# A three-layer fp32 network in one launch: its schedule built with the timeline simulation switched on

## The chip, the cores and the metric

The kernel runs on one core of a Trainium2 chip, in one launch. The metric is the device time of that launch in microseconds (us), the median of several runs. The engines are called as in the profile: PE (TensorE, the matmuls) with its weight loads PEld, DVE (VectorE), ACT (ScalarE), POOL (GpSimd) and SP (SyncE), which issues DMAs.

## The reference

`x` is one batch of 512 tokens of width 1024, all in float32. Three different blocks follow each other:

- Block 1: 16 learned tokens are put in front (528 tokens). `h += 0.5 * swiglu(rmsnorm(h))`; then a mixer whose two halves read the same normed input: forgetting attention ("fox", 16 heads of 64, softmax over `q k^T / 8` plus the difference of two cumulative sums of `log_sigmoid` gates) and retention (4 heads). `h += (sigmoid(ga) * fox @ w_o_fox + sigmoid(gb) * ret @ w_o_ret) @ w_out`; then a second swiglu FFN.
- Block 2: a gMLP mixer and a Mamba2 state-space mixer (chunks of 64 tokens: `y = (C B^T * decay) xdt + C state`), gated, projected and added; then an FFN with a causal convolution of 3 taps.
- Block 3: native sparse attention ("NSA": 8 heads; a compressed branch, and two branches with a band of position biases) beside an RWKV7 recurrence (8 heads of 64: in each chunk of 64 tokens a triangular system is solved, then `state = decay * state + update`), their outputs concatenated and projected; then the convolution FFN again.

## The kernel before, in words

Everything lies feature-major in SBUF: 128 features by 512 (or 528) tokens to a tile. Each projection weight is streamed from HBM once, 128 output features at a time, by `Ctx.wunit` (L236 to L248): SP starts a DMA of 128 x 1024 floats, ACT copies it to the rounded half `wh` (L240), DVE subtracts to get the rest `wl` (L244); the pool holds two of each. `Ctx.mm3` (L250 to L252) makes each product of three matmuls, `wh*xh`, `wh*xl` and `wl*xh`. Such a streamed matmul is the kernel's bulk work and its filler: it waits only for its weights and an accumulator.

In the four FFNs there is nothing but these. In the mixers they are mixed with work in dependent chains:

- fox, per pair of heads: scores on PE (L648 to L651), a masked exponential with row sums on DVE and ACT (L653, L660), transposes on PE (L673), the split of the transposed probabilities into `fph` (ACT, L282) and `fpl` (DVE, L287), and the products with the values (PE, L679 with `fph`, L680 with `fpl`). Beside them the next heads' q and k are projected, normed (`hrs`, `hsq`: ACT L488, L489, L455) and split (`fk0h`, `fk1h`: ACT L305, L307).
- SSD (block 2), per chunk: transposes and splits (L443, L444, L1084), score products (L1076), `E` (DVE, L1109) into the product L1112, outputs and states (L1118, L1123).
- RWKV, four pairs of heads: the triangular systems in six levels of small products (`heads`, L1711; `level`), then 8 steps for each pair, 32 in all (`steps`: PE L1809, ACT L1811, PE L1816 and L1819, DVE L1824, PE L1831 and L1834, DVE L1837). A step needs the state of the last.
- NSA, 16 units of one head, one branch: scores (PE L1535, L1536), bias and row maximum (DVE L1537), exponential (ACT L1543), scaling (POOL L1547), transposes (PE L1555), split (`ph` on ACT, `pl` on DVE) and value products (PE L1560, L1561).

The program text only gives the instructions and their dependences. What sets the order on each engine is the list scheduler of the tile framework: it holds all instructions of the context, runs them through a model of the machine, and appends to each engine's in-order queue the instruction that the model finds next. So the model decides in what order a streamed matmul, a chain's product, an ACT copy and a DVE subtraction follow each other on their engines; in the trace each engine's instructions come in the order of its own queue. Which streamed matmuls may stand between which chain instructions is also bounded by dependences and by the buffers. The chain of one RWKV step in the text:

```python
nc.tensor.matmul(rr[64 * s:64 * s + 64], ml[:, s, n, :64], vs[:, s, n], start=True, stop=True)  # L1809
nc.scalar.activation(rs_, rr, AF.Copy)                                                          # L1811
nc.tensor.matmul(sa[h], xt[h, n], rs_[h], start=True, stop=True)                                # L1819
nc.vector.tensor_copy(vs[:64, s, n], sa[64 * s:64 * s + 64])                                    # L1824
nc.tensor.matmul(ds[:, 64 * s:64 * s + 64], bk[:, s, n], vs[:, s, n], start=True, stop=True)    # L1834
nc.vector.tensor_add(s0, ds.rearrange("p (s d) -> p s d", s=2), s0)                             # L1835
nc.vector.tensor_mul(to, s0, wend[:, :, n:n + 1].to_broadcast([64, 2, 64]))                     # L1837
```

## Time and profile before

| what | value |
|---|---|
| median of 3 runs (lowest, highest) | 3429.2 us (3425.64, 3435.23) |
| profiled execution: its own time, its span | 3428.05 us, 3426.2 us |
| mean granted clock of PE | 0.988 |
| busy share PE, PEld | 97%, 79% |
| busy share DVE, ACT, POOL | 56%, 41%, 21% |
| DMA | 298.61 MB, 87 GB/s |

The span is the time from the first to the last instruction of the profiled execution; the 1.85 us between it and that execution's own time lie outside the instructions. PE's busy time counts each matmul from its start to a modelled end, and neighbours overlap, so a stretch in which PE is busy throughout can still hold more or fewer matmuls per microsecond: the distance from one start to the next tells that. The stages by time, from PE's instructions: FFN 1 to about 390 us, fox and retention to about 1110, FFN 2 to 1462, block 2's mixer to about 2064, FFN 3 to about 2494, RWKV about 2587 to 2867, NSA to 3031, the output projection and FFN 4 to the end.

### The profile page before, as it was taken

Reading aid. Unit: us, or ns where it says so; the run is one execution under the profiler, and the core shown is the slowest. Engines: PE = TensorE matmul, PEld = TensorE weight load, DVE = VectorE, ACT = ScalarE, POOL = GpSimd, SP = SyncE. Lnnn points to the kernel's source line nnn. Section 1 sums busy time; section 2 is a strip of 40 time slices with the busy share of each in tenths; the row PEclk is TensorE's granted clock in tenths of the full one; section 3 lists DMA queues with packets and bytes.
Section 4 is the critical chain, followed back from the end, with each engine's and each line's share of the span. In section 5 each row is a group of like instructions: output and inputs, shape, how many; then the busy total and the mean of one; then the engine's idle time right before and its main releaser. Section 6 shows DMA issues by size and latency. Waiting matters only on the chain. (4 is left out here: it accounts for less than half of the span.)

```text
span 3426.2 us, 48101 instructions
## 1 busy us (share of the span) xinstructions
PE 3309.6 (97%) x19089; PEld 2717.3 (79%) x19089; DVE 1932.8 (56%) x3242; ACT 1404.0 (41%) x2474; POOL 712.4 (21%) x748
## 2 busy tenths in 40 slices
PE   8999999999999999999999999999999998999999
PEld 8999977778877888876777778788876766778887
DVE  4433366655754433268777564566446656766642
ACT  3222366653433322235555233444333434754431
POOL 2110133332122111112121231111113222421100
PEclk9999999999999999999999999999999999999999
DMA  3223222232223232323332322223331012122332
GB/s 120 90 93 88 86 85 78 69 97 95 66 86 102 92 99 90 96 94 85 106 100 86 111 81 98 92 93 98 104 115 34 31 46 87 41 64 96 98 101 91
DMA packets 89601, 298.61 MB, mean 87 GB/s; under 512 B 10711, under 2 KB 11351, under 8 KB 89120
## 3 DMA queue, kind: packets, MB, share of 16 engines
q1 hardware_dynamic: 76896, 260.70, 23.7%
q0 software_dynamic: 6416, 23.80, 2.4%
q10 hardware_dynamic: 6064, 11.03, 1.0%
q8 instruction: 150, 2.46, 0.3%
q14 instruction: 75, 0.61, 0.1%
HBM read 288.02 MB, written 7.47 MB: 86 GB/s over the span
## 5 line engine op out<-in xcount | busy, mean ns | idle before, releaser
L250 PE MATMUL mm<-zh,wh 128*128 128x512 f32 (+1 forms) x3296 | 1189.8, 361 | 20.2 <-ACT zh L291 8.4
L252 PE MATMUL mm<-zh,wl 128*128 128x512 f32 (+1 forms) x3296 | 1189.0, 361 | 3.8 <-DVE wl L244 3.7
L251 PE MATMUL mm<-zl,wh 128*128 128x512 f32 (+1 forms) x3296 | 1180.2, 358 | 3.1 <-DVE zl L292 3.1
L240 ACT ACTIVATE wh<-w 128x1024 fp32r<-128x1024 f32 (+2 forms) x523 | 523.8, 1001 | 1086.6 <-PE mm L251 759.0
L244 DVE TENSOR_TENSOR wl<-w,wh 128x1024 fp32r<-128x1024 f32 (+2 forms) x523 | 627.6, 1201 | 400.1 <-ACT wh L240 392.3
L250 PEld LDWEIGHTS mm<-zh,wh 128*128 128x128 f32 x3296 | 622.8, 189 | 115.6 <-issue 10.6
L251 PEld LDWEIGHTS mm<-zl,wh 128*128 128x128 f32 x3296 | 623.6, 189 | 100.6 <-DVE zl L292 4.1
L252 PEld LDWEIGHTS mm<-zh,wl 128*128 128x128 f32 x3296 | 622.6, 189 | 100.2 <-DVE wl L244 6.9
L250 PE MATMUL mm<-hh,wh 128*128 128x512 f32 (+1 forms) x880 | 308.5, 351 | 0.0
L251 PE MATMUL mm<-hl,wh 128*128 128x512 f32 (+1 forms) x880 | 308.3, 350 | 0.0
L252 PE MATMUL mm<-hh,wl 128*128 128x512 f32 (+1 forms) x880 | 307.6, 350 | 0.0
L251 PEld LDWEIGHTS mm<-hl,wh 128*128 128x128 f32 x880 | 165.6, 188 | 23.3
L250 PEld LDWEIGHTS mm<-hh,wh 128*128 128x128 f32 x880 | 165.5, 188 | 23.3
L252 PEld LDWEIGHTS mm<-hh,wl 128*128 128x128 f32 x880 | 165.6, 188 | 23.1
L382 POOL TENSOR_TENSOR ta<-ta,rs 128x264 f32<-128x264 f32 (+1 forms) x66 | 86.0, 1316 | 395.8 <-ACT ta L381 395.8
L334 POOL TENSOR_TENSOR acc<-acc,ta 128x512 f32<-128x512 f32 (+1 forms) x49 | 85.2, 1739 | 345.7 <-ACT ta L333 345.3
L1000 POOL TENSOR_TENSOR cv<-cv 128x512 f32<-128x512 f32 x44 | 57.6, 1309 | 434.0 <-DVE cv L981 397.6
L981 DVE SCALAR_TENSOR_TENSOR cv<-ta,vec,cv 128x510 f32<-128x510 f32 (+1 forms) x176 | 132.0, 753 | 3.2 <-ACT cv L978 0.3
L384 DVE TENSOR_TENSOR tb<-mm,ta 128x264 f32<-128x264 f32 (+1 forms) x66 | 32.8, 519 | 141.5 <-PE mm L252 137.7
L380 DVE TENSOR_TENSOR ta<-mm,rs 128x264 f32<-128x264 f32 (+1 forms) x66 | 32.5, 518 | 108.3 <-PE mm L252 108.3
L995 DVE TENSOR_TENSOR ta<-mm,rs 128x512 f32<-128x512 f32 x88 | 60.3, 687 | 57.9 <-PE mm L252 57.8
L282 ACT ACTIVATE hh<-cv 128x512 fp32r<-128x512 f32 x44 | 27.8, 632 | 144.7 <-POOL cv L1000 144.7
(592 smaller groups left out, 4645.3 us busy)
## 6 DMA issues: line engine op xcount, KB each, us to landing
w<-in_w_up_dram SPq DMA_DIRECT2D x176, 512.0 KB, 3.5
w<-in_w_in_dram SPq DMA_DIRECT2D x160, 512.0 KB, 3.5
w<-in_w_dn_dram SPq DMA_DIRECT2D x64, 512.0 KB, 3.5
w<-in_w_dn_dram SPq DMA_DIRECT2D x32, 384.0 KB, 3.1
w<-in_w_out_dram SPq DMA_DIRECT2D x16, 512.0 KB, 3.5
aB<-acum_d POOLq DMA_DIRECT2D x16, 512.0 KB, 5.9
w<-in_w_pb_dram SPq DMA_DIRECT2D x32, 256.0 KB, 2.9
negc<-negc_d POOLq DMA_DIRECT2D x8, 528.0 KB, 4.1
```

Of the source, the lines that this page charges most:

```text
L240: nc.scalar.activation(h_, w_, AF.Copy)
L244: nc.vector.tensor_sub(l_, w_, h_.bitcast(F32))
L250: nc.tensor.matmul(ps, wh, xh, start=start, stop=False)
L251: nc.tensor.matmul(ps, wh, xl, start=False, stop=False)
L252: nc.tensor.matmul(ps, wl, xh, start=False, stop=stop)
L334: nc.gpsimd.tensor_tensor(acc, acc, q, op=ALU.add)
L380: nc.vector.tensor_mul(ta, a, rs[:, c])
L382: nc.gpsimd.tensor_tensor(ta, ta, rs[:, c], op=ALU.mult)
L384: nc.vector.tensor_mul(tb, b, ta)
L981: nc.vector.scalar_tensor_tensor(y[:, d:], x[:, :T - d], w(i), y[:, d:], op0=ALU.mult, op1=ALU.add)
L995: nc.vector.tensor_mul(x, p, rs)
L1000: nc.gpsimd.tensor_tensor(y[1], y[1], y[0], op=ALU.mult)
```

## The change

One argument is given to the context in which the whole program is built:

```diff
--- before.py
+++ after.py
@@ -2006,7 +2006,7 @@
         feed[f"in_{name}_dram"] = a
         D[name] = nc.dram_tensor(f"in_{name}_dram", a.shape, mybir.dt.from_np(a.dtype), kind="ExternalInput").ap()
     out = nc.dram_tensor("out_0_dram", (8, 128, 512), F32, kind="ExternalOutput").ap()
-    with tile.TileContext(nc) as tc:
+    with tile.TileContext(nc, schedule_with_timeline_sim=True) as tc:
         program(tc, D, vec, out)
     act_tables(nc)
     r = run_bass_kernel_spmd(nc, [feed], core_ids=[0])
```

It changes the model that the list scheduler runs: a timeline simulation of the engines takes the place of the default one. No tile, pool, dependence, shape or operation differs. PE has 15806 rows of instructions before and 15812 after (neighbours that differ in nothing but a slice are one row). Of PE's 17413 instructions 7022 stand at another place than before, of DVE's 3244 2106, of ACT's 2374 1474, of POOL's 753 223, and of SP's 536 4, each by one place. In the four FFNs the order on PE is the same. The consecutive stretches of streamed matmuls (L250 to L252) on PE, counted over the whole program as runs, go from 451 to 269: in fox from 149 to 102, in SSD from 46 to 58, in RWKV from 110 to 24, in NSA from 67 to 9.

The first place is ACT at the end of a fox head. `fph` are the probabilities' high halves for which L679 waits, `hrs` and `hsq` belong to the norm of a later head, `fk` is that head's k, `wh` a weight tile. Before:

```order
L488 ACTIVATE hrs_6860<-s_6861,eps0_291 128x512
L282 ACTIVATE fph_6883<-t_6878 128x512
L489 ACTIVATE hrs_6860<-hrs_6860 128x512
L282 ACTIVATE fph_6893<-t_6889 128x384
L455 ACTIVATE hsq_6722<-hrs_6860 128x512
L240 ACTIVATE wh_7028<-w32_7027 128x1024
L282 ACTIVATE fph_6902<-t_6899 128x256
```

After:

```order
L240 ACTIVATE wh_7247<-w32_7246 128x1024
L282 ACTIVATE fph_6883<-t_6878 128x512
L282 ACTIVATE fph_6893<-t_6889 128x384
L488 ACTIVATE hrs_6860<-s_6861,eps0_291 128x512
L489 ACTIVATE hrs_6860<-hrs_6860 128x512
L455 ACTIVATE hsq_6722<-hrs_6860 128x512
L305 ACTIVATE fk0h_6748<-fqt_6638 64x528
L307 ACTIVATE fk0h_6748<-fqt_6638 64x528
L305 ACTIVATE fk1h_6754<-fqt_6638 64x528
L307 ACTIVATE fk1h_6754<-fqt_6638 64x528
L282 ACTIVATE fph_6902<-t_6899 128x256
L282 ACTIVATE fph_6910<-t_6908 128x128
```

Before, one `hrs` or `hsq` instruction stands between two `fph`, a weight copy right ahead of `fph_6902`, and the `fk` copies are already done. After, a weight copy of a later tile goes ahead of `fph_6883`, and the norm's three instructions and the four `fk` copies all stand between `fph_6893` and `fph_6902`.

The second place is PE in the triangular systems of RWKV (L1711; L1654, L1657 and L1630 belong to the features of a later pair, `mm_22344` is streamed work). Before:

```order
L250 MATMUL mm_22344<-zh2_21318,wh_22346 128x512
L251 MATMUL mm_22344<-zl2_21319,wh_22346 128x512
L1711 MATMUL s_22088<-xt_21768,ys0_22062 64x32 x8
L1711 MATMUL s_22097<-xt_21784,ys1_22075 64x32 x8
L252 MATMUL mm_22344<-zh2_21318,wl_22347 128x512
L250 MATMUL mm_22344<-zh3_21328,wh_22346 128x512
L251 MATMUL mm_22344<-zl3_21329,wh_22346 128x512
L1711 MATMUL t_22108<-id64_21502,xt_21768 64x64 x8
L1711 MATMUL t_22118<-id64_21502,xt_21784 64x64 x8
```

After:

```order
L1711 MATMUL t_22064<-x0_21767,ls_22060 64x32 x8
L1711 MATMUL t_22077<-x1_21783,ls_22073 64x32 x8
L1711 MATMUL s_22088<-xt_21768,ys0_22062 64x32 x8
L1711 MATMUL s_22097<-xt_21784,ys1_22075 64x32 x8
L1711 MATMUL t_22108<-id64_21502,xt_21768 64x64 x8
L1654 MATMUL s_22130<-acc_21514,w2a_21506 128x512
L1711 MATMUL t_22118<-id64_21502,xt_21784 64x64 x8
L1657 MATMUL s_22133<-acc_21514,w2a_21506 128x512
L1711 MATMUL t_22154<-x0_21767,ls_22150 64x32 x8
```

The streamed matmuls that stood among the small products are gone from here: 40 of them (`mm_22026` and `mm_22344`) now come ahead of the first L1711 of the stage. Of the 31 distances from one step's L1819 to the next, 3 hold no streamed matmul before, and 21 after. In the last steps of the stage 72 streamed matmuls now stand that came in the NSA stage before (`mm_25061`, `mm_25149`, `mm_25260`).

The third place is PE in an NSA unit (`ph`, `pl` and `p` are the unit's probabilities, `mm_26631` is streamed work of the output projection). Before:

```order
L250 MATMUL mm_26631<-nh4_21485,wh_26633 128x512
L251 MATMUL mm_26631<-nl4_21486,wh_26633 128x512
L1583 MATMUL o_26347<-pch_25985,vcd11_24511 128x512
L252 MATMUL mm_26631<-nh4_21485,wl_26634 128x512
L1560 MATMUL o_26148<-ph_26155,v01_24517 128x512
L1535 MATMUL s_26219<-kh01_24515,qs1_25794 128x512
L1536 MATMUL s_26219<-kl01_24516,qs1_25794 128x512
L250 MATMUL mm_26631<-nh5_21487,wh_26633 128x512
L1561 MATMUL o_26148<-pl_26156,v01_24517 128x512
```

After:

```order
L1560 MATMUL o_26148<-ph_26155,v01_24517 128x512
L1535 MATMUL s_26219<-kh01_24515,qs1_25794 128x512
L1536 MATMUL s_26219<-kl01_24516,qs1_25794 128x512
L1561 MATMUL o_26148<-pl_26156,v01_24517 128x512
L1555 MATMUL t_26171<-cst_247,p_25988 128x128 x2
L1560 MATMUL o_26148<-ph_26165,v01_24517 128x384
L1583 MATMUL o_26347<-pch_25985,vcd11_24511 128x512
L1561 MATMUL o_26148<-pl_26166,v01_24517 128x384
L1560 MATMUL o_26148<-ph_26174,v01_24517 128x256
```

The streamed matmuls have left the units: before, 40 of the 64 L1561 stand ahead of the stage's last streamed matmul, after, none; of the 64 L1535 groups 51 before, 9 after. The stage holds 203 streamed matmuls before and 144 after.

## Rows read from the trace of the kernel before

**Rows 1.** The page, busy time of each engine, share of the span, instructions

```profile
PE 3309.6 (97%) x19089; PEld 2717.3 (79%) x19089; DVE 1932.8 (56%) x3242; ACT 1404.0 (41%) x2474; POOL 712.4 (21%) x748
```

**Rows 2.** Windows: us, then busy of PE, PEld, DVE, ACT, POOL, clock, DMA, GB/s

```profile
...
592.18:630.64 38.46, 36.38 (x227) 30.50 (x227) 25.85 (x61) 24.44 (x55) 14.62 (x25) 1.00 0.24 78
1204.00:1290.00 86.00, 86.00 (x376) 70.21 (x375) 34.20 (x39) 24.09 (x30) 14.37 (x8) 1.00 0.30 97
1462.00:1862.00 400.00, 378.81 (x1833) 294.68 (x1832) 300.76 (x419) 211.19 (x404) 79.95 (x63) 0.97 0.31 93
...
```

**Rows 3.** Timeline of PE in a dense FFN: start, us, engine, instruction

```profile
...
3200.31 0.39 PE L250 MATMUL mm<-zh,wh 128*128 128x512 f32 x1
3200.53 0.39 PE L251 MATMUL mm<-zl,wh 128*128 128x512 f32 x1
...
```

**Rows 4.** Timeline of PE, streamed matmuls among the RWKV ones

```profile
...
2821.66 0.50 PE L250 MATMUL mm<-zh,wh 128*128 128x512 f32 x1
2822.00 0.39 PE L251 MATMUL mm<-zl,wh 128*128 128x512 f32 x1
...
2822.69 0.39 PE L251 MATMUL mm<-zl,wh 128*128 128x512 f32 x1
2823.01 0.34 PE L1809 MATMUL o<-h,ml 128*64 128x64 f32 x4
...
```

**Rows 5.** The waits of PE in fox: us in total, times, longest

```profile
...
PE o L680 <- DVE fpl L287: 7.5, 12, 1.2
...
PE o L679 <- ACT fph L282: 4.7, 13, 0.5
...
```

**Rows 6.** ACT by form in one fox head: count, busy, mean ns, idle before

```profile
L240 ACT ACTIVATE wh<-w 128x1024 fp32r<-128x1024 f32 x4 | 4.3, 1063 | 1.1 <-PE mm L251 1.1
...
L305 ACT ACTIVATE fk0h<-fqt 64x528 fp32r<-64x528 f32 x1 | 0.6, 643 | 1.4 <-DVE fqt L593 1.4
...
```

**Rows 7.** The waits of PE in the SSD and gMLP stage

```profile
...
PE o L1112 <- DVE E L1109: 8.0, 3, 3.1
...
PE t L443 <- ACT tb L282: 7.2, 5, 2.4
...
```

**Rows 8.** Windows of the RWKV stage, columns as in Rows 2

```profile
...
2587.09:2867.18 280.09, 262.74 (x3254) 188.43 (x3254) 175.71 (x430) 108.58 (x274) 80.74 (x109) 0.96 0.13 40
2790.00:2820.00 30.00, 29.66 (x580) 24.20 (x578) 12.79 (x42) 14.40 (x42) 12.09 (x22) 1.00 0.24 75
2850.00:2860.00 10.00, 6.75 (x65) 4.69 (x64) 5.46 (x26) 4.90 (x18) 0.00 (x0) 1.00 0.17 49
2860.00:2870.00 10.00, 5.83 (x45) 4.18 (x44) 8.65 (x19) 5.26 (x12) 5.21 (x4) 0.52 0.11 28
2870.00:2880.00 10.00, 10.00 (x44) 6.45 (x43) 4.01 (x10) 3.70 (x8) 1.26 (x1) 0.79 0.13 34
...
```

**Rows 9.** Timeline of PE at the RWKV entry, with the idle time before

```profile
...
2587.09 1.96 PE L1711 MATMUL s<-ar,b 64*64 64x128 f32 x32 [1.72 <-POOL b L1689]
...
2593.23 0.68 PE L1711 MATMUL t<-id,xt 64*64 64x64 f32 x16 [2.60 <-DVE xt L1724]
...
```

**Rows 10.** The waits of PE in the RWKV steps

```profile
...
PE o L1831 <- DVE h L1824: 4.8, 8, 1.1
...
PE o L1809 <- DVE h L1837: 3.1, 4, 1.7
...
PE o L1819 <- ACT rsb L1811: 2.5, 3, 1.7
...
```

**Rows 11.** Windows of the NSA stage, columns as in Rows 2

```profile
...
2867.18:3030.70 163.52, 147.57 (x740) 110.89 (x741) 119.33 (x362) 102.50 (x268) 56.82 (x90) 0.95 0.15 51
2912.00:3030.70 118.70, 104.28 (x551) 79.50 (x551) 89.46 (x292) 80.85 (x226) 45.98 (x78) 0.96 0.10 35
...
```

**Rows 12.** PE by form in the NSA units, 2912 to 3030.7 us

```profile
...
L250 PE MATMUL mm<-nh,wh 128*128 128x512 f32 x24 | 9.9, 414 | 0.0
L1560 PE MATMUL o<-ph,v 128*128 128x512 f32 x16 | 8.7, 542 | 3.2 <-ACT ph L282 2.9
...
```

## The prediction, made before the changed kernel ran

> **What bounds the kernel now.** I read the page's busy times first, then windows stage by stage, then PE's timeline and its list of waits. PE is busy 3309.6 us, 97% of the span, and no other engine comes to 60% [rows 1]; so the span is PE's queue, and what is not PE's is about 117 us of idle time (3426.2 - 3309.6). The change takes nothing out of PE's queue and puts nothing in. It can gain only where PE stands still or where its matmuls follow each other more slowly than they could, and it can lose by adding such places.
>
> In the FFNs neither exists: a window of one holds 86.00 us of PE in 86.00 [rows 2], and streamed matmuls start 0.23 us apart [rows 3]. The order there is unchanged, so I cost these stages at nothing. All the movement is in the mixers. There a second loss hides in the busy time. In the run of streamed matmuls between two small ones in RWKV, the first holds PE 0.34 us until the next start and the last 0.32, while the two between go at 0.23 [rows 4]. So a run of streamed matmuls costs about 0.11 + 0.09 = 0.20 us beyond its matmuls, wherever one starts and ends. There are 451 such runs before and 269 after.
>
> [...]
>
> **The change part by part.** Everything is set against the profiled execution: 3428.05 us, a span of 3426.2 and 1.85 outside. It lies 1.15 us under the median of the runs shown.
>
> Fox, 8 pairs of heads. One pair takes 38.46 us, of which PE is idle 38.46 - 36.38 = 2.1 [rows 2]; the waits are for `fpl` and `fph`, in all 7.5 us in 12 and 4.7 in 13, none over 1.2 [rows 5]. In the new order a weight copy of 1.06 us goes ahead of the first `fph`, and four `fk` copies of 0.64 us, 2.6 in all, stand before the third [rows 6]. L679 and L680 are queued behind one another on PE, and behind them the filler that could have covered the wait. Walking the two queues by these durations I get PE waits of 0.55 (the accumulator's copy, late by the same queue), 0.55, 1.0, 0.8 and 2.45 us, 5.35 in place of 2.1: +3.3 for each pair. Against it stand 149 - 102 = 47 fewer runs at 0.20 us, 9.4 us or 1.2 for a pair. That is +2 for a pair, **+16 us**. Bounds: -10 (the runs saved, no new wait) and +30 (the waits, and only the bubbles of the runs that lie beside no wait).
>
> SSD and gMLP. PE is idle 400 - 378.81 = 21 us here [rows 2], of which 8.0 lie before L1112 and 7.2 before L443 [rows 7]. The first group of chunks gets its filler better spread, the second stands with almost none in its first three chunks; runs rise from 46 to 58, 12 x 0.20 = +2.4. I take **-4 us**, some of the 15 us of these two waits covered less the runs, and keep -20 (all covered and a little more) and +15 (the same waits again in the second group).
>
> RWKV, 280.09 us, of which PE is idle 17 [rows 8]. Four pieces:
> 110 - 24 = 86 fewer runs at 0.20: -17.2. The forty streamed matmuls that now stand ahead of the first L1711 (9.2 us) give POOL's `b` and DVE's `xt` the time for which PE waited 1.72 and 2.60 us [rows 9]: -4.3. The 72 streamed matmuls that come into the last steps fill the two windows where PE is busy 6.75 and 5.83 of 10 us, 7.4 us idle [rows 8]: -7.4. On the other side, 21 - 3 = 18 more steps have no streamed matmul in them. The waits inside a step are 10.4 us in 15 now (4.8, 3.1, 2.5), 0.7 each [rows 10]. But in the new order small products of the next pair still stand between, and the window at 2790, which has ten streamed matmuls among 580 instructions and is busy 29.66 of 30 us, shows that these alone nearly suffice [rows 8]. I take half a wait, 0.4 us a step: +7.2. Together **-22 us**. Bounds: -41, if the steps lose nothing and a run saves 0.34 instead of 0.20; and +66, if in each of the 18 the longest waits seen all come (1.1 + 1.7 + 1.7, and one more of 0.8 at the ends, 5.3 x 18 = 95, less the 29 saved).
>
> NSA, 163.52 us, 118.7 of it 16 units at 7.42 us [rows 11, 12]. The units hold 72 streamed matmuls, 16.6 us at 0.23 or 1.03 a unit: without them a unit is 6.4 us. DVE is busy 89.46 us in the units, 5.6 for each: the floor. The 58 runs that vanish save up to 0.7 a unit, but the chain's own waits come bare. I take 6.25 us, so 16 x 6.25 = 100, and the 144 streamed matmuls that remain, nearly all ahead of the chain, 33 us: 133, and 4 for a stretch at half clock (next paragraph), 137. Like for like (59 matmuls, 13.6 us, have left the stage) before is 163.5 - 13.6 = 150: **-13 us**. Bounds: 16 x 5.6 + 33, -27; and 16 x 7.4 + 33 + 7, +8.
>
> The clock. Between 2850 and 2870 PE's busy share falls to 67 and 58%, and the granted clock goes to 0.52, then 0.79 in the next ten microseconds of full work [rows 8]: that is 1.2 GHz for a while, at a loss of 4.8 + 2.1 = 7 us of granted clock. The mixers' own windows show 0.95 to 1.00 [rows 2, 8, 11]. This can appear wherever PE loses its filler, and here it disappears in one place and may come in another; I took 4 us of it into NSA.
> The Trainium skill ("TensorE: Matmul & The Clock Gate", section "HAM oscillation — how this bites in real kernels") says the same with a sharper edge: idle stretches that come back with each tile of work drop PE to half clock each time, so the price is paid once for each gap and not once for the stage. The trace shows one such drop here. By that rule the chain stretches without filler would be the slow case below.
>
> DVE, ACT, POOL, SP. They work as much as before; SP's DMA issues move by one place, and with DVE busy only 34.20 of 86 us in an FFN [rows 2] I cost that at nothing.
>
> Sum: +16 - 4 - 22 - 13 = -23. The span becomes 3403.2, the time **3405 us**.
>
> **The rivals.**
> First, slower: the filler was cover, and without it the chains stand bare. The place is the 18 RWKV steps. A clean step takes some 6.7 us (the window at 2790); at the pace of the window at 2850, where PE is busy 63% instead of 99, it takes 3.8 us more. Half of that, 2.0 a step, is 36 us, less the 29 saved +7; with fox at +16, SSD at -4 and NSA at its upper bound of +8 it makes +27, 3455 us. It decides from the point where a bare step costs (23 + 7)/18 = 1.7 us instead of 0.4. For it: 21 of 31 steps bare. Against it: in the window at 2790 small work alone keeps PE at 99%.
>
> Second, it cancels: fox at +30, SSD at 0, RWKV at -22, NSA at -8 (units of 6.55 us). That is 0, 3428 us. For it: fox's `fph` queue is the plainest change that I can read, and the gains are sums of small pieces.
>
> Third, a larger gain: DVE-bound NSA units (-27), RWKV without new waits (-36, near its bound), SSD -4, fox +5 since its filler slides into the waits. Together -62, 3366 us. [...] Against it: in the units PE waits for ACT and POOL as well, 3.2 us on the first `ph` alone [rows 12].
>
> That the change does nothing is out: the orders differ.
>
> **How the numbers follow.** My forecast 0.43, the slow rival 0.25, the cancelling one 0.17, the large gain 0.15. About 0.3% (10 us) is what a measurement of this kernel can tell from no change. The forecast's own range is 3388 to 3418. Faster is the forecast and the large gain, less 0.01 for a forecast that comes out just short: 0.57. Within 0.3% is the cancelling case, 0.17. Slower is the slow rival and the 0.01: 0.26. The range goes from a little beyond the large gain to the slow rival, **3355 to 3455**; beyond it lie RWKV at its upper bound and fox and NSA both at theirs.
>
> **What would show it.** Right: in the fox pair a longest wait of PE on `fph` of about 2.5 us in place of 0.5, and the pair at 40.5 us; RWKV with PE idle under 15 us and no long wait at its entry; the stretch of bare NSA units at 6.2 to 6.3 us each, with no streamed matmul in it; FFNs unchanged to the microsecond. Wrong: a granted clock near 0.5 over much of the NSA units or of the RWKV steps; PE waits on `vs` (L1824) or the state (L1837) two or three times as long as now; fox waits that stay where they are, since then the model put each instruction where the chip has it ready.

## The result and the profile after

The changed kernel takes 3510.8 us (median of 4 runs, 3506.18 to 3513.02) against 3429.05: 1.0237 times the time before, 95% interval 1.0224 to 1.025. The profiled execution's span grew from 3426.2 to 3507.1 us. The forecast was 3405 in a range of 3355 to 3455, so direction and range were both missed.

The page's busy times after, and its row of the granted clock over 40 slices, to be held against [rows 1]:

```profile
PE 3342.9 (95%) x19089; PEld 2763.0 (79%) x19089; DVE 1949.0 (56%) x3242; ACT 1399.5 (40%) x2474; POOL 698.5 (20%) x748
...
PEclk9999999989989999999999999999998877999999
```

The same 19089 matmul records take 33 us more of PE, and PE stands still for 164 us and not 117. The clock, which was at 9 tenths or more in each of the 40 slices before, dips in fox and over the stretch of RWKV and NSA.

Stage by stage, from the start times of PE's instructions. I split each stage by adding up, over the trace, the time from each matmul's start to the next one's start. "Idle" is the time from the end of all matmuls so far to the next start, where that is more than 0.1 us; "streamed" is the rest behind an L250, L251 or L252, "small" the rest behind all others. A matmul with such a gap behind it is thus counted to its modelled end, and one without it only to its neighbour's start, so that more gaps also raise "small" or "streamed".

| stage (ends with) | before | after | difference | idle | streamed (matmuls) | small |
|---|---|---|---|---|---|---|
| start to fox (first L626) | 446.8 | 446.1 | -0.7 | -5.4 | +5.8 | -0.5 |
| fox (last L756) | 295.7 | 321.5 | **+25.8** | +12.9 | -0.3 (1051 to 1032) | +13.1 |
| retention, first part (last L820) | 197.1 | 200.4 | +3.3 | -8.0 | +12.1 (1046 to 1101) | -0.8 |
| rest of retention, FFN 2, start of block 2 (first L1164) | 576.0 | 574.5 | -1.5 | +6.3 | -8.5 | +0.7 |
| SSD (last L1118) | 331.7 | 321.8 | **-9.8** | -7.1 | -0.4 | -2.4 |
| gMLP (last L1285) | 188.2 | 184.7 | -3.5 | +1.5 | -3.6 | -1.4 |
| FFN 3 to RWKV's features (first L1654) | 535.3 | 528.9 | -6.4 | -3.3 | -3.1 | 0.0 |
| features (first L1711) | 16.4 | 23.2 | +6.8 | -2.3 | +9.1 (48 to 88) | 0.0 |
| RWKV (last L1819) | 289.7 | 344.4 | **+54.7** | +35.2 | -10.4 (325 to 344) | +29.9 |
| NSA (last L1561) | 152.5 | 165.1 | **+12.6** | +15.8 | -15.1 (203 to 144) | +12.0 |
| projection, FFN 4 | 392.7 | 392.2 | -0.5 | +1.5 | -2.0 | 0.0 |
| sum | | | +80.8 | +47.1 | -16.3 | +50.6 |

So 47 us are new idle time and 51 us lie behind small matmuls, while the streamed ones became cheaper, as fewer runs should make them. Streamed matmuls that change their stage carry 0.23 us each with them [rows 3]; with that taken off, fox lost 30.2 us, RWKV 50.3 and NSA 26.2.

Of the small column's growth in these three (13.1, 29.9 and 12.0 us) 11.1, 10.6 and 7.8 us are matmuls with a gap behind them, of which there are 32, 52 and 47 in place of 2, 12 and 26: time of the same waits, by the way of counting. The small matmuls that others follow without a gap take 2.0, 19.3 and 4.2 us more. In RWKV 813 of those start while the clock is at 0.50, 0.090 us apart on average, and 2110 while it is at 1.00, 0.054 apart; before, 112 started at 0.50.

Three windows of the kernel before that were not shown, fox, RWKV up to its last L1819, and NSA (columns as in Rows 2):

```profile
446.80:742.50 295.70, 281.54 (x1707) 231.42 (x1704) 194.54 (x462) 184.72 (x412) 106.38 (x193) 1.00 0.24 78
...
2587.10:2876.70 289.60, 271.81 (x3295) 194.47 (x3297) 178.74 (x438) 112.19 (x282) 83.18 (x111) 0.95 0.13 40
...
2876.70:3029.20 152.50, 138.20 (x701) 104.69 (x701) 115.75 (x352) 97.72 (x257) 54.38 (x87) 0.97 0.16 53
```

And of the changed kernel: fox, SSD, RWKV, NSA, then four windows of 10 us inside RWKV:

```profile
446.10:767.60 321.50, 294.18 (x1687) 243.25 (x1686) 197.03 (x460) 185.69 (x413) 103.45 (x192) 0.93 0.22 74
1542.50:1864.30 321.80, 309.70 (x1556) 241.03 (x1555) 256.11 (x358) 184.57 (x370) 64.56 (x54) 0.99 0.32 96
2601.10:2945.50 344.40, 291.00 (x3321) 221.80 (x3320) 187.03 (x439) 117.17 (x290) 77.52 (x113) 0.82 0.11 34
2945.50:3110.60 165.10, 134.79 (x638) 100.96 (x636) 109.72 (x341) 94.03 (x249) 50.71 (x85) 0.92 0.13 44
...
2650.00:2660.00 10.00, 5.81 (x96) 5.38 (x96) 9.84 (x14) 2.25 (x6) 6.86 (x5) 0.50 0.01 2
2720.00:2730.00 10.00, 4.25 (x64) 3.91 (x65) 8.96 (x16) 3.25 (x9) 5.42 (x5) 0.50 0.00 1
2800.00:2810.00 10.00, 4.46 (x76) 4.24 (x76) 9.82 (x17) 2.47 (x7) 7.05 (x6) 0.50 0.01 2
2810.00:2820.00 10.00, 9.09 (x29) 4.02 (x30) 3.07 (x11) 3.17 (x7) 0.00 (x0) 0.50 0.00 2
```

RWKV's clock is 0.82 against 0.95, NSA's 0.92 against 0.97. The pattern in three of the short windows repeats: DVE is busy 9 to 10 of 10 us, PE 4 to 6, and the clock is 0.50 (1.2 GHz); in the window at 2810 it is still there although PE is busy 9 of 10 us again. Counted over the trace, the clock stands at 0.50 in 28 stretches, 246 us in all, against 18 and 82 us before; in RWKV in 8 stretches and 126 us against 5 and 27. The waits of PE in RWKV after:

```profile
PE o L1809 <- DVE h L1837: 13.2, 9, 3.2
PE o L1831 <- DVE h L1824: 11.3, 7, 5.1
PE o L1819 <- DVE xt L1755: 4.9, 1, 4.9
PE s L1711 <- POOL ys L1744: 2.9, 3, 1.2
```

Against [rows 10] the waits for the state (L1837) went from 3.1 to 13.2 us and those for L1824 from 4.8 to 11.3. Where the idle time lies can be read step by step. Of the 31 distances from one step's L1819 to the next, 22 in this trace hold no streamed matmul (21 in the queues), and they hold 32.8 us of idle time, 1.5 each; before, 3 such distances held 6.9. The steps with streamed matmuls in them hold 8.1 us as before (8.0), and the stretch ahead of the first step 11.9 against 2.8.

Two of the long waits show what PE waits for. DVE around 2660 us, ahead of the first step:

```profile
2651.40 2.31 DVE L1677 TENSOR_TENSOR_SCAN fx<-chunk,lw 128x512 f32<-128x512 f32 x1
2653.64 1.18 DVE L1683 TENSOR_SCALAR ar<-kk 128x8 f32<-128x8 f32 x1
2654.73 0.67 DVE L1681 SCALAR_TENSOR_TENSOR ar<-kk,ec 128x504 f32<-128x504 f32 x1
2655.32 2.81 DVE L1774 COPY wend<-ec 64x4 f32<-64x4 f32 x4
...
2659.29 1.82 DVE L1773 COPY ml<-ar 64x512 f32<-64x512 f32 x2
...
2662.68 0.29 DVE L1755 TENSOR_TENSOR xt<-s,xt 128x128 f32<-128x128 f32 x1
```

and PE at the same time:

```profile
2656.16 1.92 PE L1711 MATMUL s<-xt,ys 64*64 64x32 f32 x32
2663.03 0.48 PE L1819 MATMUL o<-rsb,xt 64*64 64x64 f32 x4 [4.94 <-DVE xt L1755]
2663.29 1.92 PE L1711 MATMUL s<-ar,b 64*64 64x128 f32 x16
2665.14 0.79 PE L250 MATMUL mm<-zh,wh 128*128 128x512 f32 x1
2665.73 0.63 PE L251 MATMUL mm<-zl,wh 128*128 128x512 f32 x1
2666.16 0.63 PE L252 MATMUL mm<-zh,wl 128*128 128x512 f32 x1
2666.59 0.49 PE L250 MATMUL mm<-zh,wh 128*128 128x512 f32 x1
```

The products for L1755 end at 2658.08. L1755, 0.29 us long, runs at 2662.68, behind features and operands of the next pair that DVE has ahead of it in its queue. L1819 waits for it 4.94 us with nothing else to do: the streamed matmuls stand behind it and one L1711 group in PE's queue, too late to fill the wait. When they come, the second and third start 0.43 us ahead of the next and not 0.23 [rows 3]; the clock stood at 0.50 since 2649.7.

Inside a step without streamed matmuls it is the same. PE, then DVE, at 2805 us:

```profile
2804.82 1.86 PE L1711 MATMUL s<-xt,ys 64*64 64x32 f32 x32
2810.17 0.47 PE L1831 MATMUL o<-lrb,h 64*64 64x64 f32 x2 [3.48 <-DVE h L1824]
```

```profile
2806.64 1.81 DVE L1773 COPY ml<-ar 64x512 f32<-64x512 f32 x2
2808.47 0.75 DVE L1694 SCALAR_TENSOR_TENSOR bo<-r,vec,k 128x512 f32<-128x512 f32 x1
2809.14 0.85 DVE L1773 COPY ml<-ar 64x512 f32<-64x512 f32 x2
2809.91 0.47 DVE L1824 COPY h<-o 64x64 f32<-64x64 f32 x2
```

The L1819 whose result L1824 copies starts at 2804.58; the copy runs at 2809.91, behind DVE's bulk work for the next pair.

### The profile page after: what moved, and what is told of

Read it like the earlier page. It is cut to its first block, busy times and chain, and to the rows that moved or that the text cites. A ratio compares the mean times of both kernels' runs of the same rounds, so it can differ in the third digit from the quotient of the medians.

```text
span 3507.1 us, 48161 instructions
## 1 busy us (share of the span) xinstructions
PE 3342.9 (95%) x19089; PEld 2763.0 (79%) x19089; DVE 1949.0 (56%) x3242; ACT 1399.5 (40%) x2474; POOL 698.5 (20%) x748
## 5 line engine op out<-in xcount | busy, mean ns | idle before, releaser
L250 PE MATMUL mm<-zh,wh 128*128 128x512 f32 (+1 forms) x3296 | 1187.3, 361 | 28.3 <-ACT wh L240 8.8
L252 PE MATMUL mm<-zh,wl 128*128 128x512 f32 (+1 forms) x3296 | 1187.2, 361 | 12.6 <-DVE wl L244 12.5
L251 PE MATMUL mm<-zl,wh 128*128 128x512 f32 (+1 forms) x3296 | 1176.6, 357 | 2.8 <-DVE zl L292 2.7
L244 DVE TENSOR_TENSOR wl<-w,wh 128x1024 fp32r<-128x1024 f32 (+2 forms) x523 | 637.7, 1220 | 418.7 <-ACT wh L240 411.6
L250 PEld LDWEIGHTS mm<-zh,wh 128*128 128x128 f32 x3296 | 623.7, 189 | 125.5 <-ACT wh L240 10.8
L252 PEld LDWEIGHTS mm<-zh,wl 128*128 128x128 f32 x3296 | 623.4, 189 | 113.2 <-DVE wl L244 15.9
L251 PEld LDWEIGHTS mm<-zl,wh 128*128 128x128 f32 x3296 | 625.4, 190 | 102.7 <-DVE zl L292 4.6
L250 PE MATMUL mm<-hh,wh 128*128 128x512 f32 (+1 forms) x880 | 308.1, 350 | 0.0
L251 PE MATMUL mm<-hl,wh 128*128 128x512 f32 (+1 forms) x880 | 308.0, 350 | 0.0
L252 PE MATMUL mm<-hh,wl 128*128 128x512 f32 (+1 forms) x880 | 306.5, 350 | 0.0
L251 PEld LDWEIGHTS mm<-hl,wh 128*128 128x128 f32 x880 | 165.6, 188 | 23.1
L250 PEld LDWEIGHTS mm<-hh,wh 128*128 128x128 f32 x880 | 165.6, 188 | 23.1
L252 PEld LDWEIGHTS mm<-hh,wl 128*128 128x128 f32 x880 | 165.2, 188 | 23.4
L981 DVE SCALAR_TENSOR_TENSOR cv<-ta,vec,cv 128x511 f32<-128x511 f32 (+1 forms) x176 | 132.2, 752 | 3.5 <-ACT cv L978 0.6
L384 DVE TENSOR_TENSOR tb<-mm,ta 128x264 f32<-128x264 f32 (+1 forms) x66 | 32.8, 519 | 136.8 <-PE mm L252 134.3
L380 DVE TENSOR_TENSOR ta<-mm,rs 128x264 f32<-128x264 f32 (+1 forms) x66 | 32.6, 519 | 106.0 <-PE mm L252 105.8
L250 PE MATMUL mm<-ybh,wh 128*128 128x512 f32 x192 | 76.9, 402 | 1.6 <-ACT ybh L282 1.6
```

Of the source, the lines that this page charges most:

```text
L244: nc.vector.tensor_sub(l_, w_, h_.bitcast(F32))
L250: nc.tensor.matmul(ps, wh, xh, start=start, stop=False)
L251: nc.tensor.matmul(ps, wh, xl, start=False, stop=False)
L252: nc.tensor.matmul(ps, wl, xh, start=False, stop=stop)
L384: nc.vector.tensor_mul(tb, b, ta)
L981: nc.vector.scalar_tensor_tensor(y[:, d:], x[:, :T - d], w(i), y[:, d:], op0=ALU.mult, op1=ALU.add)
```

## The experiments

All of them pin queues: the order in which each engine's instructions stand is recorded from a first build with one model, the program is traced again with the other, and the recorded order is imposed on chosen engines over chosen stages by edges that wait for nothing:

```diff
+    for e in ENGINES:
+        row = [real[k] for k in order if str(real[k].engine).endswith(e) and ...]
+        for s in STAGES:
+            lo, hi = MARK[s]
+            pos = [p for p, i in enumerate(row) if lo <= rank[i.name] < hi]
+            a, b = pos[0], pos[-1]
+            for x in row[:a]:
+                after(row[a], x)
+            for p in range(a, b):
+                after(row[p + 1], row[p])
+            for x in row[b + 1:]:
+                after(x, row[b])
+    order = build(arrays, False)[2]
+    nc, feed, _ = build(arrays, True, order)
```

Kernels below that pin the changed kernel's own order have its stage times outside RWKV (fox 319.0 to 320.6 us against 321.5), so pinning by itself costs nothing that shows.

**One engine's queue at a time.** `pe_before`: `STAGES = ["whole"]`, `ENGINES = ["PE"]`, recorded with the default model, built with the timeline model.

> The timeline model schedules, but PE's whole queue is pinned to the order of the kernel before; ACT, DVE and POOL are ordered by the model around it. Theory 1, the loss sits in PE's queue (streamed matmuls gathered into long runs ahead of the chains, so that PE has nothing to do while a chain waits): the 82 us come back, 3420 to 3440 us, and RWKV takes some 290 us and not 344. Theory 2, the loss sits in the queues of DVE, ACT and POOL (chain instructions late behind other work of their engine): 3490 to 3515 us, RWKV 330 us or more.

Measured: 3527.4 us, 1.0284 (1.0267 to 1.0301). `pe_after`: the same with the two models exchanged.

> The mirror image: the default model schedules, but PE's whole queue is pinned to the order of the changed kernel. Theory 1 (PE's queue): 3490 to 3515 us, as slow as the changed kernel. Theory 2 (the other queues): 3430 to 3450 us.

Measured: 3580.9 us, 1.0441 (1.0425 to 1.0456). Both are slower than both kernels and outside the ranges of both theories: theory 1 and theory 2 fall. RWKV's window in the first and in the second:

```profile
2631.90:2965.10 333.20, 293.89 (x3297) 209.00 (x3297) 182.28 (x436) 113.99 (x283) 81.21 (x111) 0.86 0.12 36
```

```profile
2655.20:3013.40 358.20, 293.30 (x3319) 222.60 (x3320) 183.75 (x444) 118.84 (x291) 78.74 (x113) 0.81 0.10 33
```

PE's queue of before, with the other queues made by the timeline model around it, still leaves 333 us and a clock of 0.86. Its steps have their streamed matmuls back, and yet those steps hold 19.6 us of idle time (8.0 before) and the stretch ahead of the first step 12.3: streamed work in PE's queue alone does not cover the waits that the other queues make. In both mixtures PE's queue was worth less than with the partners it was made with.

**One stage, all queues.** `s_rwkv` and `s_mix`: `ENGINES` all four; `STAGES = ["rwkv"]`, and `["mixer1", "rwkv", "nsa"]`.

> The changed kernel with all four engines' queues pinned to the order of before from the first to the last instruction of RWKV, the rest free. If RWKV's loss (+55 us from its first L1711 to its last step, +62 from its first feature product) is its own: 3511 - 62 to 3511 - 50 = 3449 to 3461 us. If the streamed matmuls that are pinned back into RWKV are missed elsewhere (a fixed stock of filler, and who has it does not matter): 3485 us or more, with fox or NSA longer by what RWKV gains.

> The changed kernel with all four queues pinned to the order of before in block 1's mixer (fox and retention), in RWKV and in NSA; block 2's mixer and the boundaries stay as the timeline model orders them, where the changed kernel was faster by 10 us in SSD, 4 in gMLP and 6 in the stretch up to RWKV. If the stages add up: 3511 - 29 - 62 - 13 = 3407 us (3400 to 3415), faster than both kernels. If the gains of block 2 hang on the order around it: 3425 to 3435 us.

Measured: 3603.5 us, 1.0506 (1.0488 to 1.0524), and 3486.2, 1.0169 (1.0154 to 1.0184). Both missed, because the pinned stretch was too wide: one early constant of RWKV stands at DVE's seventh place, so DVE was pinned almost from the program's start. It is a third case of the same finding: in `s_rwkv` RWKV itself came back (291.5 us), but fox, with DVE's queue from one model and PE's from the other, took 361.3 us against 295.7 and 321.5; in `s_mix` fox, RWKV and NSA came back and SSD took 360.8 us against 331.7 and 321.8. With the pinned stretch starting where a stage's instructions stand close together:

```diff
+            pos = [p for n, p in enumerate(pos) if pos[min(n + 20, len(pos) - 1)] - p < 60]
```

> As s_rwkv, but the pinned stretch now begins on each engine where RWKV's instructions stand close together; in s_rwkv one early constant of RWKV stood at DVE's seventh place, so that DVE's queue was pinned almost from the start of the program while PE, ACT and POOL were free. Theory J (the order of the four queues belongs together: each is good only with the others it was made with): with all four pinned in RWKV alone, 3511 - 62 to 3511 - 50 = 3449 to 3461 us, the stretch from the first L1711 to the last L1819 near 290 us. Theory S (a fixed stock of filler): 3485 us or more, the loss turning up in NSA or fox.

> As s_mix with the same tight bounds: all four queues as before in block 1's mixer, RWKV and NSA, as the timeline model orders them elsewhere. Theory J: the stages add up, 3511 - 29 - 62 - 13 = 3407 us (3400 to 3418), faster than both kernels by what SSD, gMLP and the stretch up to RWKV gained. Theory S, or gains of block 2 that hang on their neighbours: 3425 us or more.

Measured: 3451.5 us, 1.0071 (1.0056 to 1.0086), and **3412.1 us, 0.9957 (0.9943 to 0.9971)**, the shortest time of all kernels here, by 0.4% under the one before. Both lie in the ranges that theory J named. RWKV's window in `rwkv_tight`:

```profile
2599.30:2888.00 288.70, 270.24 (x3295) 193.09 (x3297) 179.19 (x438) 112.19 (x282) 82.98 (x111) 0.96 0.13 40
```

The stage takes 288.7 us, as long as before (289.7) and at its clock, and the kernel gets back 59 us of 82. The mirror image, the changed kernel's order in RWKV alone under the default model (`rwkv_mirror`):

> The mirror of rwkv_tight: the default model schedules, and all four queues are pinned to the order of the changed kernel in RWKV alone. Theory J (a stage's loss belongs to its joint order): 3429 + 50 to 3429 + 62, 3479 to 3491 us, with RWKV at about 344 us and the small matmuls in it at about 200 us of PE's time. If RWKV's loss needed the changed stretch ahead of it (weights or DVE work that come late into it): RWKV under 320 us, below 3465 us.

Measured: 3482.3 us, 1.0158 (1.0141 to 1.0175), and

```profile
2589.10:2933.30 344.20, 291.02 (x3321) 221.84 (x3320) 186.88 (x439) 117.17 (x290) 77.63 (x113) 0.82 0.11 34
```

which is the changed kernel's RWKV in every column to within 0.2 us, with its 53 us of idle time and 201 us of small matmuls. Theory J's forecasts hold both ways: RWKV's loss belongs to the joint order of the four queues in that stage, and the stages nearly add up (a neighbour can move by some us: NSA takes 146.1 us here against 152.5). Which of the four queues carries the loss no run shows, since none exchanges one queue within RWKV alone.

**Are the streamed matmuls cover?** `thin_before` and `thin_after` pin all queues to one kernel's order and shorten L252 for RWKV's weights, which leaves a part of that product out:

```diff
-        nc.tensor.matmul(ps, wl, xh, start=False, stop=stop)
+        n = 32 if PRIO["on"] and "rwkv" in MARK and "rwkv_end" not in MARK else ps.shape[1]
+        nc.tensor.matmul(ps[:, :n], wl, xh[:, :n], start=False, stop=stop)
```

> The order of before on all four queues, but of each streamed product of RWKV's weights the third matmul (L252, 152 of them) runs over 32 columns and not 512, so a part of that product is left out; 152 x 0.23 = 35 us of streamed matmuls go, some 25 us of them within RWKV. Theory C (cover: in the order of before the streamed matmuls stand where PE would wait for a step, in the changed order they stand in long runs apart from the waits): before gets shorter by clearly less than 35 us, 10 to 25. Rival (the streamed matmuls are paid in full in both orders, and the waits of the changed order come from elsewhere): 33 to 36 us, 3393 to 3396 us.

> The same thinning in the order of the changed kernel, all four queues pinned to it. Theory C: it gets shorter by nearly all of the 35 us, 28 to 38: 3473 to 3483 us, and so the two orders lie further apart than 82 us. Rival: 33 to 36 us in both, a distance of 82 us as without thinning.

Measured: 3427.7 us, 1.0003 (0.9989 to 1.0018), and 3497.6, 1.0208 (1.0193 to 1.0223). Both miss the ranges of theory C and of its rival. The size in the expectation was wrong. PE in `thin_before`:

```profile
2701.60 0.50 PE L251 MATMUL mm<-zl,wh 128*128 128x512 f32 x1
2701.93 0.18 PE L253 MATMUL mm<-zh,wl 128*128 128x32 f32 x1
2701.96 0.48 PE L250 MATMUL mm<-zh,wh 128*128 128x512 f32 x1
2702.28 0.40 PE L251 MATMUL mm<-zl,wh 128*128 128x512 f32 x1
```

(L253 is the shortened matmul; its line has moved by one.) The next start follows it after 0.03 us, but the one after that 0.32 later and not 0.23, so 0.11 us goes for each, some 17 us for 152 (an estimate). (The expectation's last clause also had its sign wrong: the two must come closer.) Of 17 us the changed order gives back 13.3, the order before 0 within its interval, and RWKV's window there is

```profile
2583.70:2872.20 288.50, 270.01 (x3297) 198.48 (x3297) 178.70 (x438) 111.94 (x282) 84.11 (x111) 0.89 0.13 40
```

against 289.7. So in the order before taking this work out gains nothing. But the reason is not theory C's. Had the streamed matmuls only filled waits, idle time would have grown by what was taken out. By the split used above, streamed time in RWKV falls by 9.7 us, idle time rises by 0.6 and the small matmuls take 7.9 more: the clock fell from 0.95 to 0.89 (64 us at 0.50 and not 27) with the work taken out. That filler covers waits is not shown by this pair of runs; what it shows is that here the clock took back what the shorter work gave. Whether PE would bound the stage at an unchanged clock stays open.

**What the clock costs.** `fill1`, `fill2` and `fill_half` keep the changed kernel's order and put dummy matmuls in front of the instructions at which PE stood still:

```diff
+                junk(K, "rr", 8 * t + c, w)
+    nc.tensor.matmul(w[:, 256:], z[:, :128], z[:, 256:512], start=True, stop=True)  # FILL[place, step] times
```

> The changed kernel with all four queues pinned to its own order, and 267 dummy matmuls (128 x 256 elements, 0.12 us each, into a part of the step's accumulator that nothing reads) put on PE right ahead of the L1809, L1819 and L1831 before which the changed kernel's PE stood still in RWKV: 20 places, 31.7 us of waits, each filled with about its own length. Theory K (a good part of RWKV's +55 us is the granted clock, 0.82 there against 0.95 before, and it falls because PE stands still): the clock in RWKV rises to 0.88 or more and the kernel gets shorter by 10 to 25 us, 3486 to 3501 us, although PE has 32 us more to do. Rival W (only the waits count, the clock falls where PE waits anyway): 3505 to 3515 us, RWKV at 344 us; with some dummies paid, more.

> The same at double length: 528 dummy matmuls, 63 us, half of them more than the waits hold. Theory K: the clock is at least as high as with the single dose, and of the second 32 us a part is paid: 3500 to 3522 us. Rival W: the second dose is paid in full, 3535 to 3547 us.

> The same 20 places with 131 dummies, 16 us at full clock: the first dose overran the waits, since a dummy placed where the clock is at its lower level takes about twice its 0.12 us. In the single dose PE's small matmuls in RWKV took 17.7 us less than in the changed kernel (183.2 against 200.9), the idle time 17.6 us less, and the streamed and dummy matmuls 46 more. Theory K (small matmuls are slow because the clock is low, and PE's idle time lowers it): idle time falls by some 16 us, the small matmuls by some 10, the dummies cost some 20: 3500 to 3508 us, with more work than the changed kernel. Rival W: 3508 to 3516 us.

Measured: 3515.2 us, 1.0246 (1.0228 to 1.0263); 3533.7, 1.0301 (1.0285 to 1.0316); 3510.8, 1.0239 (1.0218 to 1.0259). Split as in the table above, RWKV by dose:

| dummies | RWKV | clock | idle | streamed and dummies | small |
|---|---|---|---|---|---|
| 0 | 344.4 | 0.82 | 52.9 | 90.4 | 201.1 |
| 131 | 347.2 | 0.85 | 39.4 | 116.4 | 191.3 |
| 267 | 355.2 | 0.88 | 35.3 | 136.6 | 183.3 |
| 528 | 368.6 | 0.94 | 32.6 | 160.8 | 175.2 |
| order before | 289.7 | 0.95 | 17.7 | 100.8 | 171.2 |

Theory K forecast a gain and there is none, at any dose; as a forecast of time it falls, and rival W's times came closer (3510.8 lies in its range, 3515.2 at the edge of it, 3533.7 just under it). But what theory K says of the clock is in the columns: each dose lifts it and takes 10 to 26 us off the same small matmuls, of their +29.9. Counting only those without a gap behind them, they take 187, 179, 173 and 165 us by dose, and 168 in the order before. The dummies cost more than they give (26, 46 and 70 us, for 23, 35 and 46 us of idle time and small matmuls): they start 0.12 us apart at the full clock, but 0.21 at 0.50, where 113 of the 267 are followed by another one. At these places and doses, empty work does not buy back what the clock costs.

## Why the prediction was wrong

**"So the span is PE's queue."** This premise of the first part let the other queues drop out of RWKV's sum. PE's busy share was read as a bound; `pe_before` has PE's whole queue of before and takes 3527 us, and taking some 17 us of streamed work out of the order before (`thin_before`) gains nothing. DVE's busy share, 34.20 of 86 us, was taken from an FFN; in the RWKV windows at 0.50 in which PE waits it is 9 to 10 of 10 us.

**FFNs at nothing.** Right: FFN 4 with the projection went from 392.7 to 392.2 us.

**The 0.20 us for a run.** Right as a mechanism, smaller in size: with 182 runs fewer, 36 us by that price, the streamed time fell by 16. In RWKV it fell by 10.4 with 19 more matmuls (4.4 us), so 14.8 against 17.2 forecast. No run takes the runs of streamed matmuls apart from the rest, so the price itself stays an estimate.

**Fox, +16.** Right in sign; +25.8 lies within its bounds, the +30.2 without the 19 streamed matmuls that left at the upper one. The waits behind the `fph` queue came only in part. After:

```profile
PE o L679 <- ACT fph L282: 10.2, 10, 2.0
PE o L680 <- DVE fpl L287: 7.7, 13, 2.0
PE mm L250 <- DVE fqt L587: 5.4, 4, 2.9
```

The longest wait on `fph` went from 0.5 [rows 5] to 2.0 us (forecast 2.5), but the total on `fph` rose by 5.5 us and that on `fpl` by 0.2, and idle time by 12.9 against 26 in the working. As much as on `fph`, 5.2 us, came from streamed matmuls that wait for DVE's `fqt`, which no term had; before it was

```profile
PE mm L250 <- DVE fqt L587: 0.2, 1, 0.2
```

Of the 13.1 us in the small column 11.1 stand ahead of waits, as said above. The run saving of 9.4 did not show.

**SSD and gMLP, -4.** Right in sign: -9.8 and -3.5. The waits of [rows 7] on L1112 and L443 nearly went; SSD's idle time fell from 19.0 to 11.9 us.

**RWKV, -22; measured +54.7**, and +50.3 without the 19 streamed matmuls that came into it. This is the step that failed, at "I take half a wait, 0.4 us a step". It took the window at 2790, where small work alone kept PE busy, for what all 18 bare steps would look like. In that window DVE is busy 12.79 of 30 us [rows 8]; in the new order it is full where the chain needs it. Idle time rose by 35.2 us: 26 in the bare steps, 1.4 for each of the 18 that were added, and 9.1 ahead of the first step. With the slower small matmuls the steps together take 282.4 us in place of 244.9, with 13 streamed matmuls fewer (3.0 us), which is 2.2 for each of the 18. The entry gained less than the 4.3 us of [rows 9]: 23.2 us with 40 more matmuls (9.2) against 16.4, -2.4 like for like, and the wait for DVE's `xt` (L1724) went from 2.6 to 0.8, but the other waits ahead of the first step cost more than that.

**NSA, -13; measured +12.6**, but the forecast was made like for like, without the 59 streamed matmuls (13.6 us) that left the stage, and by that count it is +26.2. A unit without filler was to take 6.25 us. The L1583 of the kernel before stand from 2915.5 to 3009.5 (94.0 us, 94 streamed matmuls among them), those after from 2998.6 to 3093.6 (95.0, with 24), so the units take as long with little filler as with it: streamed time between them fell by 18.8 us, idle time rose by 7.6 and the small column by 12.1, at a clock of 0.93 in place of 0.98. Here the filler did stand in waits, at least in part; how much of it the clock took back no run separates. Like for like 17.1 of the 26.2 us are here. Another 11.8 lie ahead of the units: from the last L1819 to the first L1583 it takes 53.1 us and not 38.8, with 11 more streamed matmuls (2.5 us) and 9.8 us of idle time in place of 1.5. (The end of the stage gained 2.7.) The waits on `ph` before:

```profile
PE o L1560 <- ACT ph L282: 4.0, 7, 2.5
```

And after, with two that were shorter or not there (5.3 us of the second is one wait, between RWKV's end and the first streamed matmul of the stage):

```profile
PE o L1560 <- ACT ph L282: 9.9, 11, 2.5
PE mm L250 <- DVE x L1901: 5.5, 2, 5.3
PE o L1561 <- DVE pl L287: 4.3, 14, 0.7
```

**The clock, 4 us.** Far too small: small matmuls that others follow without a gap took 19.3 + 2.0 + 4.2 = 25.5 us more in RWKV, fox and NSA, most of it at 0.50 in RWKV. The Trainium skill ("TensorE: Matmul & The Clock Gate", section "HAM oscillation — how this bites in real kernels") says that the price comes back with each gap. The trace agrees that it comes back: the three stretches at 0.50 that begin at 2649.7, 2714.6 and 2796.5 have 1.2 to 1.4 us of idle PE in the 8 us ahead of them and longer waits inside. The prediction saw one such drop and weighed the rest only inside a rival; the trace before holds 18, 5 of them in RWKV and 6 in SSD. What grew in RWKV is less their number, 5 to 8, than the time at 0.50, 27 to 126 us.

**The rivals.** The first one happened: bare chains and a lower clock. It was priced at 3455 us, with a chance of 0.25; its own threshold, 1.7 us for a bare step, was passed at 2.2. (Its 63% is the mean of the windows at 2850 and 2860; the one at 2850 shows 67%.) It fell short in RWKV, +7 against +50.3 like for like: the savings of 29 us came only in part, and the stretch ahead of the first step lost 9.8 us. It also fell short in fox, where it had no price of its own, and by NSA's upper bound of +8, which had nothing for the stretch ahead of the units but 7 us of lower clock. The large gain and the cancelling case did not come.

**The signs named.** Of those for "wrong", two came: clocks near 0.5 in RWKV, and waits on L1824 and L1837 two to four times as long. Of those for "right", the longest wait on `fph` came nearly (2.0 us), but a fox pair takes 42.3 us from one L626 to the next (37.5 before, 40.5 forecast), and `fph` explains only part of that; that fox's forecast had the right sign is in part luck.

What stays open: why the model orders DVE's bulk work ahead of the short links, and whether DVE's queue alone, put back within RWKV, would bring the stage back. No run shows either.

## What to carry to other kernels

Before an order's streamed work is priced, shorten it where it stands and see if the time moves, and look at the clock as well: here it fell with the work. A high busy share of PE does not say that PE's queue alone decides: with the same matmuls in fewer, longer runs, and DVE's bulk work ahead of short links, RWKV took 55 us more. Read the waits by step, and look at what the releasing engine had ahead of the link in its queue. Where two schedules of the same program differ by stage, build the mix with all queues of a stage taken together: here the default order in fox, retention, RWKV and NSA and the timeline order elsewhere beat both, by 0.4% and 2.8%, at 3412 us.

## What the runs showed of the hardware that I had not expected

A streamed matmul cut from 512 to 32 columns between full ones saves 0.11 us and not 0.20: the next start comes 0.03 us behind it, but the one after that 0.32 us later and not 0.23. At the lower clock streamed matmuls start 0.43 us apart. Taking work out can lower the clock: 108 streamed matmuls cut to 32 columns took RWKV from 0.95 to 0.89 in the order before. And 528 dummy matmuls lift the granted clock of a 345 us stage from 0.82 to 0.94 and make other matmuls 26 us faster, without making the stage shorter.
